# A sparse 3x3 convolution on one core: from a planned order to a hand-synchronised program with a loop on TensorE

## The chip, the cores and the metric

The kernel runs on one core of a Trainium2 chip. The metric is device time in microseconds of one execution. A core has TensorE (PE in the profile; its weight loads are PEld), VectorE (DVE), ScalarE (ACT), GpSimd (POOL) and SyncE (SP), each with its own instruction stream, and 16 DMA engines that all the transfers share. Engines wait for each other through semaphores. PSUM is the memory that TensorE writes, in eight banks of 2 KB a partition; SBUF is the working memory.

## The reference

A convolution of 16 images of 64 channels, 64 x 64 pixels, with 128 filters of 3 x 3, padded by one pixel, in fp32. A tenth of the weights are not zero, but the zeros lie at random.

```python
batch, c_in, h, w, c_out, k = 16, 64, 64, 64, 128, 3
x_pad = np.pad(x, ((0, 0), (0, 0), (pad, pad), (pad, pad)), mode='constant')
for b in range(batch):
    for co in range(c_out):
        for ci in range(c_in):
            for kh in range(k):
                for kw in range(k):
                    if weight[co, ci, kh, kw] != 0:
                        output[b, co] += weight[co, ci, kh, kw] * x_pad[b, ci, kh:kh+h, kw:kw+w]
```

## The kernel before

It treats the convolution as a dense one, in bf16 with fp32 sums. Two images are a pair: their 2 x 64 channels fill the 128 partitions, and the two halves of TensorE's rows work on one image each, side by side. So each step of the multiplication is two matmuls of 64 rows, one for each image.

A pair's 64 rows are cut into four blocks of 16 rows. A block of kind T (`twos`) saves a third of the work by sharing between two neighbouring rows of output. Write G0, G1, G2 for the three rows of taps. For output rows r and r+1, the sum x[r] + x[r+1] times G1 is needed by both; the even row adds x[r+1] times (G2 - G1) and x[r-1] times G0, the odd row adds x[r] times (G0 - G1) and x[r+2] times G2. So a block needs three products: shared (3 taps across), even (6) and odd (6), 15 pairs of matmuls on 8 rows of 64 columns. The first block of all is direct (D): 18 pairs, with no sum to wait for.

The engines share the work so: POOL adds the two rows (L169), TensorE multiplies (L150), ACT copies the shared product out of PSUM to `pc` (L176), and DVE adds it to the even and the odd product, once for each image, into the output tile `o` (L183). Tiles come from pools: eight PSUM tiles of one bank, three `s`, four `pc`, three `o`. A planner puts in the waits; the order on each engine is that in which the code is written (`manual_schedule`). The program is straight: TensorE has 989 matmuls and as many weight loads in its stream. Where a row above or below the image is wanted, the matmul is made one row shorter (441 or 448 columns instead of 504 or 512).

The start: SP loads the weights (L60) and the first 32 rows of pair 0 in fp32 (L62, `x_head`). DVE and ACT cast the weights to bf16 and the head too (L101), TensorE transposes the weights, and DVE forms the two differences. Idle matmuls fill TensorE's time before.

Loads of the other pairs are issued by POOL, which casts them to bf16 in the transfer (L63, L68). Up front go the rest of pair 0, pairs 1 to 3 and 24 rows of pair 4; the rest follow from inside the block loop, after the last sum of pairs 1 to 5, beside the stores. Stores are issued by SP as each pair is done (L207), the last pair's in two halves (L205). After pair 1's store five tiny loads of one weight (`spare`, L211) follow on SP.

Of the kernel before, what the change touches and what calls it, by code (L numbers as in the profile page):

```python
# [12 lines left out]

BLOCKS = {p: "TTTT" for p in range(8)}
BLOCKS[0] = "DTTT"  # L20


G0, G1, G2, G21, G01 = range(5)
KW_ORDER = (1, 0, 2)


@with_exitstack
def kernel(
# [7 lines left out]

# [4 lines left out]
    HEAD = 32  # L41

    const_pool = ctx.enter_context(tc.tile_pool(name="const", bufs=1))
    x_pool = ctx.enter_context(tc.tile_pool(name="x", bufs=1))
    s_pool = ctx.enter_context(tc.tile_pool(name="s", bufs=3))
    p_pool = ctx.enter_context(tc.tile_pool(name="pc", bufs=4))
    o_pool = ctx.enter_context(tc.tile_pool(name="o", bufs=3))
    psum_pool = ctx.enter_context(
        tc.tile_pool(name="psum", bufs=8, space=bass.MemoryType.PSUM)
    )  # L50

    ctx.enter_context(tc.manual_schedule())


# [3 lines left out]
    xs = [x_pool.tile([128, H, W], BF16, name=f"x{p}") for p in range(NP)]  # L58
    w_sb = const_pool.tile([C_OUT, C_IN * KH * KW], FP32, name="w_sb")
    nc.sync.dma_start(out=w_sb, in_=weight.rearrange("o i kh kw -> o (i kh kw)"))  # L60
    x_head = const_pool.tile([128, HEAD, W], FP32, name="x_head")
    nc.sync.dma_start(out=x_head, in_=pair(0)[:, 0:HEAD, :])  # L62
    nc.gpsimd.dma_start(out=xs[0][:, HEAD:H, :], in_=pair(0)[:, HEAD:H, :])  # L63
    ident = const_pool.tile([128, 128], BF16, name="ident")
    make_identity(nc, ident)

    def load(p, a=0, b=H):
        nc.gpsimd.dma_start(out=xs[p][:, a:b, :], in_=pair(p)[:, a:b, :])  # L68

    EARLY, CUT = 4, 24

    LATER = {2: (5,), 3: (6,), 4: (7, 0, 32), 5: (7, 32, 64)}
    for p in range(1, EARLY):
        load(p)
    load(EARLY, 0, CUT)


    idle_rhs = const_pool.tile([128, 512], BF16, name="idle_rhs")  # L80
    nc.vector.memset(idle_rhs, 0.0)  # L81
    idle_ps = psum_pool.tile([128, 512], FP32, name="ps")

    def keep_busy(n):
        for _ in range(n):
            nc.tensor.matmul(idle_ps, idle_rhs[:, 0:128], idle_rhs, start=True, stop=True)  # L86

    keep_busy(7)

    w_v = w_sb.rearrange("o (i k) -> o k i", k=KH * KW)
    w_bf = const_pool.tile([C_OUT, 3, 4 * C_IN], BF16, name="w_bf")
    w_bf4 = w_bf.rearrange("o g (k i) -> o g k i", k=4)
    wT = const_pool.tile([128, 5, 3, C_OUT], BF16, name="wT")
# [4 lines left out]
    def cast_x(copy, a, b):  # L100
        copy(out=xs[0][:, a:b, :], in_=x_head[:, a:b, :])  # L101

    def cast(g, copy, a, b):
        k = 3 * g + a % 3
        copy(out=w_bf4[:, g, a:b, :], in_=w_v[:, k : k + b - a, :])  # L105

    def transposed(g):
        wps = psum_pool.tile([128, 4, 128], FP32, name="ps")
        for j in range(3):
            src = w_bf[:, g, C_IN * j : C_IN * (j + 2)]  # L110
            nc.tensor.matmul(wps[:, j, :], src, ident, start=True, stop=True)  # L111
        return wps[:, 0:3, :]

    def difference(g, wps):
        nc.vector.tensor_tensor(out=wT[:, g], in0=wps, in1=wT[:, G1], op=SUB)  # L115

    cast(G1, nc.vector.tensor_copy, 0, 3)
    cast(G1, nc.scalar.copy, 3, 4)
    cast(G0, nc.vector.tensor_copy, 0, 3)
    cast(G0, nc.vector.tensor_copy, 3, 4)  # L120
    cast(G2, nc.scalar.copy, 0, 3)
    cast(G2, nc.vector.tensor_copy, 3, 4)
    cast_x(nc.vector.tensor_copy, 0, 9)
    nc.scalar.copy(out=wT[:, G1], in_=transposed(G1))
    ps0 = transposed(G0)
    nc.vector.tensor_copy(out=wT[:, G0], in_=ps0)  # L126
    ps2 = transposed(G2)
    nc.scalar.copy(out=wT[:, G2], in_=ps2)
    keep_busy(7)
    cast_x(nc.scalar.copy, 9, 18)  # L130
    difference(G01, ps0)
    difference(G21, ps2)
    cast_x(nc.scalar.copy, 18, HEAD)


    def product(terms, rows):


        ps = [psum_pool.tile([128, rows, W], FP32, name="ps") for _ in range(2)]
        todo = [(t, kw) for t in terms for kw in KW_ORDER]  # L140
        for i, ((src, g, first, step), kw) in enumerate(todo):
            n_src = src.shape[1]
            lo = 0 if first >= 0 else 1
            hi = rows if first + (rows - 1) * step < n_src else rows - 1
            c_lo, c_hi = max(0, 1 - kw), min(W, W + 1 - kw)
            a = first + lo * step
            b = first + (hi - 1) * step + 1
            for n in range(2):
                q = slice(64 * n, 64 * n + 64)
                nc.tensor.matmul(  # L150
                    ps[n][:, lo:hi, c_lo:c_hi],
                    tap(g, kw, n),
                    src[q, a:b:step, c_lo + kw - 1 : c_hi + kw - 1],
                    start=(i == 0),
                    stop=(i == len(todo) - 1),
                )
        return ps

    def direct(p, o, r0, rows):
        ps = product(  # L160
            [(xs[p], G1, r0, 1), (xs[p], G0, r0 - 1, 1), (xs[p], G2, r0 + 1, 1)], rows
        )
        nc.scalar.copy(out=o[0][:, r0 : r0 + rows, :], in_=ps[0])  # L163
        nc.vector.tensor_copy(out=o[1][:, r0 : r0 + rows, :], in_=ps[1])  # L164

    def twos(p, o, r0):
        t0 = r0 // 2
        s = s_pool.tile([128, 8, W], BF16, name="s")
        nc.gpsimd.tensor_tensor(  # L169
            out=s, in0=xs[p][:, r0 : r0 + 16 : 2, :], in1=xs[p][:, r0 + 1 : r0 + 16 : 2, :], op=ADD  # L170
        )
        shared = product([(s, G1, 0, 1)], 8)
        pc = []
        for n in range(2):
            c = p_pool.tile([128, 8, W], FP32, name="pc")
            nc.scalar.copy(out=c, in_=shared[n])  # L176
            pc.append(c)
        even = [(xs[p], G21, r0 + 1, 2), (xs[p], G0, r0 - 1, 2)]
        odd = [(xs[p], G01, r0, 2), (xs[p], G2, r0 + 2, 2)]
        for first, terms in ((r0, even), (r0 + 1, odd)):  # L180
            ps = product(terms, 8)
            for n in range(2):
                nc.vector.tensor_tensor(  # L183
                    out=o[n][:, first : r0 + 16 : 2, :], in0=ps[n], in1=pc[n], op=ADD
                )

    for p in range(NP):
        both = o_pool.tile([C_OUT, 2, H, W], FP32, name="o")
        o = [both[:, n] for n in range(2)]
        into = out[2 * p : 2 * p + 2].rearrange("n o h w -> o n h w")  # L190
        last = p == NP - 1
        for blk in range(4):
            r0 = 16 * blk
            if BLOCKS[p][blk] == "T":
# [47 lines left out]
```

## Time and profile before

| what | value |
|---|---|
| time, median of three runs | 131.87 us |
| the three runs | 126.64, 131.87, 132.14 us |
| span of the profiled execution, first to last instruction | 124.3 us |
| own total of the profiled execution | not given on the page; only the span is |
| TensorE busy | 108.7 us (87%) |
| DVE, ACT, POOL busy | 82.5, 39.0, 41.7 us |
| packets of SP's queue and of POOL's queue, share of 16 DMA engines | 67.2% and 30.7% |
| HBM read and written | 17.07 MB and 33.55 MB |

The page gives, for each group of instructions, its source line, engine, operation, output and input, count, then busy time in all, mean duration of one, and the idle time of the engine ahead of them with what ended it. The rows of tenths cut the span into 40 slices; a 9 means 90% or more. TensorE's busy time counts matmuls that overlap, so it says little of how near to its best it runs; the distance between equal steps says more.

### The profile page before, as it was taken

The numbers are of one execution on the slowest core, as the hardware profiler recorded it, in microseconds if no ns is written. First come the engines' busy times: TensorE is split into PE (matmuls) and PEld (weight loads), VectorE is DVE, ScalarE is ACT, GpSimd is POOL, SyncE is SP. The second block draws the span as 40 slices with busy tenths as digits, with TensorE's granted clock in tenths as the row PEclk, the third lists the DMA queues.
The fourth block names the chain that finished last, engine by engine and source line by source line (L and its number), as shares of the span: only waits on it lengthen the run. The fifth ranks groups of instructions, "written<-read, shape, count | busy, mean of one in ns | idle before, by whom it ended". The sixth has DMA issues, their size and how long they took to land.

```text
span 124.3 us, 2453 instructions
## 1 busy us (share of the span) xinstructions
PE 108.7 (87%) x989; PEld 57.2 (46%) x989; DVE 82.5 (66%) x135; ACT 39.0 (31%) x71; POOL 41.7 (34%) x47
## 2 busy tenths in 40 slices
PE   6959999999999999999999999999999999970000
PEld 2425555555555555555555555555555555530000
DVE  0353577877787778777877878887877787772000
ACT  4543333333333333333333333333333333330000
POOL 6409333533353335333443335333333320000000
PEclk9999999999999999999999999999999999997555
DMA  4999999999999999999999999999999999999991
GB/s 120 348 220 227 219 213 213 238 411 338 335 392 422 319 316 324 377 340 329 303 385 378 354 380 443 376 349 389 418 422 437 422 427 427 437 427 403 432 414 82
DMA packets 4198, 42.91 MB, mean 345 GB/s; under 512 B 347, under 2 KB 347, under 8 KB 1115
## 3 DMA queue, kind: packets, MB, share of 16 engines
q1 hardware_dynamic: 2746, 34.90, 67.2%
q0 software_dynamic: 1440, 7.86, 30.7%
q8 instruction: 7, 0.11, 0.3%
q14 instruction: 5, 0.03, 0.1%
HBM read 17.07 MB, written 33.55 MB: 407 GB/s over the span
## 4 chain that ended last, share of the span: by engine, by line
PE 82%; DMA 5%; DVE 1%; issue 1%; DVEq 0%; SPq 0%
PE ps L150 82%; DMA x_head<-in_x_dram 5%; DVE o L183 1%; DVEq L237 0%; DVE x L101 0%; SPq L60 0%; DVEq L183 0%
## 5 line engine op out<-in xcount | busy, mean ns | idle before, releaser
L183 DVE TENSOR_TENSOR o<-ps,pc 128x512 f32<-128x512 f32 x124 | 77.8, 686 | 22.1 <-PE ps L150 19.2
L150 PE MATMUL ps<-x,wT 64*128 64x504 bf16 (+3 forms) x780 | 88.8, 373 | 1.3 <-DVE x L101 1.3
L150 PEld LDWEIGHTS <-wT 64*128 64x128 bf16 x966 | 55.2, 94 | 49.5 <-issue 1.7
L169 POOL TENSOR_TENSOR s<-x 128x512 bf16<-128x512 bf16 x31 | 35.6, 1150 | 57.6 <-PE ps L150 41.1
L176 ACT COPY pc<-ps 128x512 f32<-128x512 f32 x62 | 33.3, 589 | 64.0 <-issue 61.8
L150 PE MATMUL ps<-s,wT 64*128 64x512 bf16 (+1 forms) x186 | 25.7, 377 | 0.0
L86 PE MATMUL ps<-idle_rhs 128*128 128x512 bf16 x14 | 4.8, 505 | 1.2 <-DVE idle_rhs L81 1.2
L68 POOL DMA_DIRECT2D x<-in_x_dram x9 | 5.0, 560 | 0.0
L86 PEld LDWEIGHTS <-idle_rhs 128*128 128x128 bf16 x14 | 1.5, 118 | 3.2 <-issue 1.4
L105 DVE CAST w_bf<-w_sb 128x192 bf16<-128x192 f32 (+1 forms) x4 | 1.1, 351 | 2.5 <-DMA w_sb<-in_weight_dram 2.5
L164 DVE COPY o<-ps 128x512 f32<-128x512 f32 x2 | 1.4, 692 | 2.0 <-PE ps L150 2.0
L101 DVE CAST x<-x_head 128x576 bf16<-128x576 f32 x1 | 0.5, 460 | 2.6 <-DMA x_head<-in_x_dram 2.6
L101 ACT CAST x<-x_head 128x576 bf16<-128x576 f32 (+1 forms) x2 | 1.5, 802 | 1.8 <-DMA x_head<-in_x_dram 1.8
L163 ACT COPY o<-ps 128x512 f32<-128x512 f32 x2 | 1.2, 586 | 2.4 <-PE ps L150 2.4
L105 ACT ACT_TABLE_LOAD x1 | 1.3, 1283 | 0.7 <-PEq L226 0.7
L105 ACT CAST w_bf<-w_sb 128x64 bf16<-128x64 f32 (+1 forms) x2 | 0.7, 416 | 1.6 <-DMA w_sb<-in_weight_dram 1.6
L115 DVE TENSOR_TENSOR wT<-ps,wT 128x384 bf16<-128x384 f32 x2 | 1.0, 548 | 0.0
L111 PEld LDWEIGHTS <-w_bf 128*128 128x128 bf16 x9 | 0.5, 97 | 1.0 <-DVE w_bf L105 1.0
L63 POOL DMA_DIRECT2D x<-in_x_dram x1 | 0.7, 693 | 0.8 <-POOLq L226 0.8
L111 PE MATMUL ps<-ident,w_bf 128*128 128x128 bf16 x9 | 0.9, 222 | 0.1
L81 DVE MEMSET idle_rhs<- 128x256 uint32 x1 | 0.3, 272 | 0.9 <-PEq L226 0.9
L126 DVE CAST wT<-ps 128x384 bf16<-128x384 f32 x1 | 0.6, 551 | 0.0
(8 smaller groups left out, 1.9 us busy)
## 6 DMA issues: line engine op xcount, KB each, us to landing
out_dram<-o SPq DMA_DIRECT2D x7, 4096.0 KB, 19.8
x<-in_x_dram POOLq DMA_DIRECT2D x5, 1024.0 KB, 16.8
out_dram<-o SPq DMA_DIRECT2D x2, 2048.0 KB
x<-in_x_dram POOLq DMA_DIRECT2D x3, 512.0 KB, 13.8
x_head<-in_x_dram SPq DMA_DIRECT2D x1, 1024.0 KB, 6.2
x<-in_x_dram POOLq DMA_DIRECT2D x1, 640.0 KB, 14.8
x<-in_x_dram POOLq DMA_DIRECT2D x1, 384.0 KB, 22.3
w_sb<-in_weight_dram SPq DMA_DIRECT2D x1, 288.0 KB
```

Source lines behind the costliest of these rows:

```text
L68: nc.gpsimd.dma_start(out=xs[p][:, a:b, :], in_=pair(p)[:, a:b, :])
L86: nc.tensor.matmul(idle_ps, idle_rhs[:, 0:128], idle_rhs, start=True, stop=True)
L101: copy(out=xs[0][:, a:b, :], in_=x_head[:, a:b, :])
L105: copy(out=w_bf4[:, g, a:b, :], in_=w_v[:, k : k + b - a, :])
L111: nc.tensor.matmul(wps[:, j, :], src, ident, start=True, stop=True)
L115: nc.vector.tensor_tensor(out=wT[:, g], in0=wps, in1=wT[:, G1], op=SUB)
L150: nc.tensor.matmul(ps[n][:, lo:hi, c_lo:c_hi], tap(g, kw, n), src[q, a:b:step, c_lo + kw - 1 : c_hi + kw - 1], start=(i == 0), stop=(i == ...
L163: nc.scalar.copy(out=o[0][:, r0 : r0 + rows, :], in_=ps[0])
L164: nc.vector.tensor_copy(out=o[1][:, r0 : r0 + rows, :], in_=ps[1])
L169: nc.gpsimd.tensor_tensor(out=s, in0=xs[p][:, r0 : r0 + 16 : 2, :], in1=xs[p][:, r0 + 1 : r0 + 16 : 2, :], op=ADD)
L176: nc.scalar.copy(out=c, in_=shared[n])
L183: nc.vector.tensor_tensor(out=o[n][:, first : r0 + 16 : 2, :], in0=ps[n], in1=pc[n], op=ADD)
```

## The change

The planner and its pools go. The whole program stands in one hand-written section, with named semaphores, and tiles with fixed addresses:

- TensorE's program becomes a loop of 16 turns over two blocks, counted by a register, with a branch at its end. Each product is preceded by waits that stand alone: `take` waits until a semaphore is at least 1 and lowers it by one. There are four for each block: `s_odd` and `s_sum` before the shared product, `s_free` before the even one, `s_even` before the odd one.
- So that all blocks look alike, the matmuls read fixed tiles. POOL still makes `sums`, and now also copies nine even rows of x (the block's and the next) to `even`; ACT copies nine odd rows (from the one above the block) to `odd`. Each tile is there twice. A row outside the image is written as zeros, so all blocks multiply full tiles. The direct first block is gone. For block 0 DVE fills both.
- PSUM: one tile of two banks for the shared product, one for the even, two in turn for the odd. ACT's copy and DVE's sums take both images in one instruction, of 1,024 elements a partition.
- The head of pair 0 stays fp32 and is loaded in two parts, 17 and 15 rows.
- Loads: POOL issues the rest of pair 0 and pairs 1 to 4 up front, and pairs 5 to 7 together after it has filled block 1's tiles.
- Stores: SP waits until pair 6 has landed (`GATE`) before the first store. Pairs 6 and 7 are stored in halves. There are four output tiles; the fourth (`home`) lies over the head and the tiles of pairs 0 to 2. The five `spare` loads are gone.

The waits of the other engines are written as counts of `s_pe`, which rises by two with each product, six with each block. The diff, cut to its core (added lines):

```diff
+    ctx.enter_context(tc.tile_critical(no_gpsimd_drain=True))
...
+    outs = [sbuf(f"o{k}", [C_OUT, 2, H, W], FP32) for k in range(3)]
+    outs.append(home.rearrange("o (n r) (h w) -> o n (r h) w", n=2, w=W))
...
+    sums = [sbuf(f"sums{k}", [128, HALF, W], BF16) for k in range(UNROLL)]
+    odd = [sbuf(f"odd{k}", [128, HALF + 1, W], BF16) for k in range(UNROLL)]
+    even = [sbuf(f"even{k}", [128, HALF + 1, W], BF16) for k in range(UNROLL)]
+    pc = [sbuf(f"pc{k}", [128, 2, HALF, W], FP32) for k in range(3)]
+    ps = [nc.alloc_psum_tensor(f"ps{k}", [128, 2, HALF, W], FP32).ap() for k in range(4)]
...
+    for i, (a, b) in enumerate(zip((0, FIRST), (FIRST, HEAD))):
+        nc.sync.dma_start(out=x_head[:, a:b, :], in_=pair(0)[:, a:b, :]).then_inc(s_head[i], 16)
...
+    fill_even(0, v, vcopy, vzero, s_dve)
+    fill_odd(0, v, vcopy, vzero, s_dve)
...
+    g = nc.gpsimd
+    for k in range(N):
+        if k >= UNROLL:
+            wait(g, s_pe, 6 * (k - UNROLL) + 2)
+        fill_sums(k)
+        if k == 0:
+            g.wait_ge(s_dve, 10)
+        else:
+            if k >= UNROLL:
+                wait(g, s_pe, 6 * (k - UNROLL) + 6)
+            fill_even(k)
+        if k == 1:
+            for p in range(UP_FRONT, NP):
+                load(p)
+
+    fill_odd(1)
+    for k in range(N):
+        wait(a, s_pe, 6 * k + 2)
+        a.copy(out=pc[k % 3], in_=ps[0]).then_inc(s_pc, 1)
+        if k + UNROLL < N:
+            wait(a, s_pe, 6 * k + 4)
+            fill_odd(k + UNROLL)
...
+    for k in range(N):
+        p, b = divmod(k, BLOCKS)
+        o = outs[p % 4]
+        r0 = ROWS * b
+        if p >= 4:
+            wait(v, s_st[p - 4], 16)
+        wait(v, s_pc, k + 1)
+        wait(v, s_pe, 6 * k + 4)
+        v.tensor_tensor(
+            out=o[:, :, r0 : r0 + ROWS : 2, :], in0=ps[1], in1=pc[k % 3], op=ADD
+        ).then_inc(s_free, 1)
+        wait(v, s_pe, 6 * k + 6)
+        v.tensor_tensor(
+            out=o[:, :, r0 + 1 : r0 + ROWS : 2, :], in0=ps[2 + k % 2], in1=pc[k % 3], op=ADD
+        ).then_inc(s_out, 1)
+
+    s = nc.sync
+    s.wait_ge(s_x[GATE], 16)
+    for p in range(NP):
...
+            s.wait_ge(s_out, BLOCKS * p + BLOCKS // parts * (h + 1))
+            s.dma_start(
+                out=into[:, :, rows * h : rows * (h + 1), :],
+                in_=outs[p % 4][:, :, rows * h : rows * (h + 1), :],
+            ).then_inc(s_st[p], 16)
...
+    def take(s):
+        t.wait_ge(s, 1).then_inc(s, -1)
...
+    nc.br("blocks", engines=[PE])
+    with nc.body("blocks", valid_engines=[PE]):
+        for k in range(UNROLL):
+            take(s_odd)
+            take(s_sum)
+            product(ps[0], [(sums[k], G1, 0)])
+            take(s_free)
+            product(ps[1], [(odd[k], G21, 1), (odd[k], G0, 0)])
+            take(s_even)
+            product(ps[2 + k], [(even[k], G01, 0), (even[k], G2, 1)])
+        t.reg_add(turn, turn, 1)
+        t.br_lt(turn, N // UNROLL, "blocks", "blocks_done")
```

## The prediction

> **What bounds the kernel now.** I read the page first, then the DMA view by stage, TensorE's timeline, and SP's waits.
>
> ```profile
> span 124.3 us, 2453 instructions
> ...
> DMA  4999999999999999999999999999999999999991
> GB/s 120 348 220 227 219 213 213 238 411 338 335 392 422 319 316 324 377 340 329 303 385 378 354 380 443 376 349 389 418 422 437 422 427 427 437 427 403 432 414 82
> ...
> q1 hardware_dynamic: 2746, 34.90, 67.2%
> q0 software_dynamic: 1440, 7.86, 30.7%
> q8 instruction: 7, 0.11, 0.3%
> ...
> PE 82%; DMA 5%; DVE 1%; issue 1%; DVEq 0%; SPq 0%
> ...
> L183 DVE TENSOR_TENSOR o<-ps,pc 128x512 f32<-128x512 f32 x124 | 77.8, 686 | 22.1 <-PE ps L150 19.2
> L150 PE MATMUL ps<-x,wT 64*128 64x504 bf16 (+3 forms) x780 | 88.8, 373 | 1.3 <-DVE x L101 1.3
> ...
> L169 POOL TENSOR_TENSOR s<-x 128x512 bf16<-128x512 bf16 x31 | 35.6, 1150 | 57.6 <-PE ps L150 41.1
> L176 ACT COPY pc<-ps 128x512 f32<-128x512 f32 x62 | 33.3, 589 | 64.0 <-issue 61.8
> ```
>
> The chain of work names TensorE for 82%, but it ends with the last instruction on a compute engine. The DMA row is the other story: nines from the second slice to the last but one. SP's waits show the end:
>
> ```profile
> SPq L237 <- DMA out_dram<-o: 10.0, 3, 4.8
> ```
>
> The last store is issued at 112.6 us and SP then waits 10.0 us for three store landings: a half store still lay ahead of it. So DMA ends the span, and TensorE (last matmul 111.2) is close behind.
>
> DMA rates by stage: the DMA view of 8 to 20 us (loads alone), then of 100 to 120 us (stores alone), then stages of 4 us, whose last two columns are the busy share and GB/s.
>
> ```profile
> DMA packets 367, 2.61 MB, mean 217 GB/s; under 512 B 47, under 2 KB 47, under 8 KB 53
> ```
>
> ```profile
> DMA packets 776, 8.47 MB, mean 424 GB/s; under 512 B 48, under 2 KB 48, under 8 KB 48
> ```
>
> ```profile
> 88.00:92.00 4.00, 4.00 (x40) 2.13 (x38) 3.27 (x6) 1.07 (x2) 1.15 (x1) 1.00 1.01 431
> ...
> 96.00:100.00 4.00, 4.00 (x42) 2.20 (x40) 3.06 (x5) 1.91 (x4) 1.92 (x2) 1.00 1.04 438
> ```
>
> A load is counted by the bf16 that it writes, so 217 GB/s is 434 GB/s of fp32 read.
>
> TensorE's pace, from its timeline: a block's shared product starts at 62.99, 66.23, 69.47, 72.63, that is 3.24 us for an inner block and 3.16 for one at an image's edge.
>
> ```profile
> 62.99 0.83 PE L150 MATMUL ps<-s,wT 64*128 64x512 bf16 x6
> 63.63 2.77 PE L150 MATMUL ps<-x,wT 64*128 64x512 bf16 x24
> 66.23 0.83 PE L150 MATMUL ps<-s,wT 64*128 64x512 bf16 x6
> ```
>
> **The change part by part.**
>
> *DMA order.* The same bytes move; no store starts before pair 6 has landed. Worked from pure rates: loads 7.86 MB / 0.217 = 36.2 us, stores 33.55 / 0.424 = 79.1, weights and head 3.6 (1.76 to 5.4 us is at a share of 1.00, and loads alone follow). Sum 118.9. First data come at 1.76, so DMA would be done at 120.7. Now it is done at about 121.8 (the stage 121.0 to 124.3 has a share of 0.24, 0.8 us). Gain 1.1 us. While SP waits for pair 6, pair 7 is still queued (1.05 MB / 0.217 = 4.8 us), more than the roughly 1 us from a store's issue to its first data (weights: issue 0.74, data 1.76), so no hole opens. The five spare DMAs go; SP's timeline has them from 36.2 to 41.1, with nothing due on SP before 48.6: 0.
>
> *Are stores there in time?* Output p is done at 8.2 + 12.96(p+1) + 1.3 (DVE's last sum), by the block time below. Pair 5: 87.3; DMA has by then loads to 41.6 and five stores of 9.9, so it wants pair 5 at 91. Pair 6's halves are done at 93.7 and 100.2, wanted at 101 and 106; pair 7's at 106.7 and 113.2, wanted at 111 and 116. Buffers: block 16 (at 60 us) overwrites output 0, stored by about 52. Enough.
>
> *TensorE's work.* Edge rows are now multiplied as zeros: 16 edge blocks go from 3.16 to 3.24. The direct first block (18 pairs of matmuls) becomes one of 15. So 32 x 3.24 = 103.7 us. The extra cost is 1.3 us for zeros less 0.6 for the first block.
>
> *The loop's waits.* Each block gets four waits that stand alone in TensorE's stream, and there are 16 branches. The trace has one such wait inside the stream: 51 ns, executed at 10.25 us, 2.2 us before the matmul it precedes (12.41), and the pair cadence of 0.216 goes on. The final drain, too, is reached 2.4 us before the last matmul ends. So the sequencer runs about ten pairs ahead and the waits cost nothing while that lead lasts. Bounds: 0, and 128 x 51 ns = 6.5 us. What the lead shrinks to depends on the last releaser. Odd tile: the block before's even product ends 1.94 into it, ACT copies 576 elements (672 ns in the x_head row), so 2.65 of 3.24; with the zero row (64 elements, 304 ns) 2.95. Even PSUM: DVE starts at 1.97 and takes two images at once (two of 686 ns overlap to 1.26, from 2.52 for four), so 3.23, wanted 0.65 into the next block. Lead 0.3 to 0.65 us, one and a half to three pairs. I take 0.5 us in all (nearest row: the 51 ns wait that cost nothing), and keep 6.5 as the end. Behind a late wait stand all further matmuls, then DVE, then the last store.
>
> *Helpers' budgets per 3.24 us.* ACT: one copy of 1024 (589 for 512 and 479 for 384 give 0.86 ns an element: 1.03 us) plus 0.67. DVE 2.5. POOL: 1.15 for the sum plus a copy of 576 elements, which the trace does not have: above, the two-input row scaled, 1.29; below, the 128-element memset, 0.22. Even with 1.29 it is 2.44. All are under 3.24, so off the path; if POOL's copy took over 2 us it would bound.
>
> *POOL's three late loads* stand between block 1's fill and block 2's sum: 3 x 0.56 = 1.7 us, from 10.2 to 11.9, then 1.15 to 13.1; wanted at 14.7. Cover 1.6 us. If an issue blocked because more is queued than before, block 2 would be late by the excess; no row shows one longer than 0.7 us.
>
> *Start.* x_head's casts (L101) become fills. DVE: weight differences end near 6.6, the two fills 0.46 and about 0.6, so 7.7. ACT needs the second head part, 7.4 as now, plus 0.67. TensorE starts at 8.2 (now 7.95). Entering the hand-written section adds a hop on SP ahead of the first DMA: 0.2 us; leaving it adds another round of drains: the round at the end now takes 0.9 after the last landing, so I add 0.4.
>
> *Sum.* TensorE ends at 8.2 + 103.7 + 0.5 = 112.4; DVE 113.7; data of the last half from 114.7 to 119.6. DMA by its own sum: 120.9. The later counts. The tail was 2.5 (121.8 to 124.3), now 2.9: span **123.8**, 0.5 us less (0.4%). Allowing half of the gap to the better DMA rates below, I forecast 0.8% less. The slack of TensorE is 1.3 us; past it each us is paid.
>
> The page gives no own total; the lowest run shown, 126.64, is 2.3 above the span, and the median, 131.87, is 7.6. I carry the ratio to the median: **130.8**.
>
> [...]
>
> **Rivals.** (1) *Unmixed traffic runs at the best stages.* Stores at 433 (77.5 us), loads at 219 (35.9), head 3.6: 117.0, done at 118.9, so TensorE then decides, at 119.6: span 122.5; with the 0.5 of the waits and the 0.4 of the way out both hidden 121.6, 2.2% less, 129.0. For: 88 to 100 us. Against: 424 over the long stretch. (2) *Waits exposed.* The lead is too short for the sequencer, and each stand-alone wait costs its 51 ns: TensorE ends at 118.4, data at 125.6, span 128.5, 3.4% more, 136.4. It costs from 1.3 us of exposure (10 ns a wait). For: the waits now empty the queue once a block; against: the wait at 10.25. [...] (4) *POOL late once*, by an issue that blocks for 3 to 5 us: span 125 to 128, about 134. (5) *The order does nothing*: stores and loads mix as well as they run apart (the 24 to 86 us stretch is busy at 1.02), span 124.7, same.
>
> **How the numbers follow.** Forecast 0.42, (5) 0.09, (1) 0.26, (2) 0.13, (3) 0.05, (4) 0.05. Faster by over 2%: 0.26; within 2% (about what a measurement of this kernel tells from nothing): 0.51; slower: 0.23. The range: up to case (2), 136.4; down to 2% under the lowest run shown, 124.1, since the median may fall at that level. The forecast's own span is 122.5 to 125.
>
> **What would show it.** Right: load-only DMA to about 42 us, then stores alone at 424 or more; TensorE's blocks 3.24 apart; an end set by the last store with the queue never empty. Wrong: gaps on TensorE at each block or each second one, a DMA share under 1 after 90 us, sums from POOL coming late at block 2.

## The result, and the profile after

| what | before | after |
|---|---|---|
| time, median of four runs each, side by side | 129.25 us | 132.09 us |
| lowest and highest run | 126.25 and 132.14 us | 130.94 and 133.41 us |
| time of the profiled execution | 126.64 us | 132.42 us |
| its span | 124.3 us | 130.7 us |
| TensorE's first product starts | 7.95 us | 14.61 us |
| last landing of a store | 123.44 us | 128.88 us |

The changed kernel is slower: the ratio is 1.042, with a 95% interval of 1.033 to 1.051. The kernel before shows its times at two levels (126.3 and 126.6, 131.9 and 132.1), and the ratio compares undisturbed runs alone, which for the kernel before are those of the lower level.

The 132.09 lies inside the range of the forecast, 124.1 to 136.4, but only because the forecast of 0.8% less was carried to the median of 131.87. Carried to the 126.64 of the profiled execution it would have been 125.6, with an upper end of 131.0 (the 3.4% of its second rival), and 132.42 came out. So the forecast was wrong, in sign and in size, and that the range held the result is luck. The span has 6.4 us to explain.

The page of the changed kernel:

```profile
span 130.7 us, 2483 instructions
...
PEclk9999559999999999999999999999999999999975
DMA  3999999999999999999999999399719999999692
GB/s 108 229 276 225 216 216 218 208 218 218 208 223 216 386 426 426 436 431 416 451 429 424 426 429 426 156 421 461 321 80 472 411 399 411 426 404 434 288 406 120
...
q1 hardware_dynamic: 3152, 34.90, 64.3%
q0 software_dynamic: 1152, 7.86, 29.0%
...
PE 81%; DVE 2%; issue 0%; DVEq 0%
...
L268 ACT COPY pc<-ps 128x1024 f32<-128x1024 f32 x32 | 32.4, 1012 | 42.0 <-PE ps L318 42.0
...
L284 DVE TENSOR_TENSOR o<-ps,pc 128x1024 f32<-128x1024 f32 x24 | 29.4, 1225 | 27.0 <-PE ps L318 27.0
...
L161 POOL COPY even<-x 128x576 bf16<-128x576 bf16 (+1 forms) x20 | 13.0, 649 | 21.4 <-PE ps L318 21.4
```

Three things are to be seen. The DMA row now has holes, from slice 26 on (82 us): before it was nines to the last slice but one. The clock row has a pair of fives in slices 5 and 6 (13 to 20 us). And the sizes that the forecast had estimated came out: ACT's copy 1.01 us (estimate 1.03), DVE's double sum 1.23 (1.26), POOL's copy 0.65 (between 0.22 and 1.29).

The loads run alone to about 42 us, the last of them lands at 46.4, and from there the stores run alone, at 416 to 451 GB/s, as was foreseen. Then the queue runs dry. That is SP's wait, by line 301, for DVE's sums; its wait for the last landings has shrunk from 10.0 us to 6.0:

```profile
SPq L301 <- DVE o L288: 53.8, 6, 12.7
...
SPq L306 <- DMA out_dram<-home: 6.0, 1, 6.0
```

So now the outputs are late, and TensorE decides the end. Its timeline (start, time from the first to the last of a group, in us; idle time ahead in brackets) shows where. The first line is the start of the kernel before, the rest is of the changed one:

```profile
7.95 3.99 PE L150 MATMUL ps<-x,wT 64*128 64x512 bf16 x36 [1.30 <-DVE x L101]
```

```profile
14.61 1.46 PE L318 MATMUL ps<-sums,wT 64*128 64x512 bf16 x6 [7.11 <-PEq L329]
15.85 2.79 PE L318 MATMUL ps<-odd,wT 64*128 64x512 bf16 x12
18.41 2.13 PE L318 MATMUL ps<-even,wT 64*128 64x512 bf16 x12
20.36 0.82 PE L318 MATMUL ps<-sums,wT 64*128 64x512 bf16 x6
...
23.60 0.82 PE L318 MATMUL ps<-sums,wT 64*128 64x512 bf16 x6
...
26.84 0.82 PE L318 MATMUL ps<-sums,wT 64*128 64x512 bf16 x6
```

The first product starts at 14.61, after 7.1 us in which TensorE did nothing. The first block takes 5.75 us (14.61 to 20.36), all others 3.24. This row of a stage gives the reason for the 5.75: the column before the last two is the granted clock, 0.56.

```profile
14.60:20.40 5.80, 5.79 (x32) 2.45 (x34) 1.23 (x1) 1.78 (x3) 3.86 (x7) 0.56 1.04 218
```

The sum is 14.61 + 5.75 + 31 x 3.24 = 120.8; DVE's last sum starts at 121.23. Against the forecast (start 8.2, 32 x 3.24, 0.5 for the waits: 112.4) this is 6.4 for the start and 2.5 for the clock, less the 0.5 that the waits did not take: 8.4. The forecast's own chain through TensorE ended with data at 119.6; 8.4 later is 128.0, and the last landing came at 128.88.

What did TensorE wait for? Not for block 0's own tiles: DVE has filled both by 10.27 us, and POOL's sum is done at 9.98. The wait named, L329, is `take`. Block 0's `take(s_odd)` is answered by ACT, and the first thing that ACT signals there is the fill of block 1's `odd` tile, which reads the odd rows 15 to 31, all but the first of them from the second part of the head. ACT's timeline, then the two parts in the view of the DMA issues (KB, us from issue to landing), then the whole head of the kernel before in the same view:

```profile
13.65 0.67 ACT L152 CAST odd<-home 128x576 bf16<-128x576 f32 x1 [7.34 <-DMA home<-in_x_dram]
```

```profile
home<-in_x_dram SPq DMA_DIRECT2D x1, 544.0 KB, 7.2
...
home<-in_x_dram SPq DMA_DIRECT2D x1, 480.0 KB, 11.7
```

```profile
x_head<-in_x_dram SPq DMA_DIRECT2D x1, 1024.0 KB, 6.2
```

So two things meet: a transfer of 480 KB that takes 11.7 us, where the whole head of 1,024 KB took 6.2 before, and a wait that is answered one block ahead. The trace's packets show why the transfer takes so long. The second part moves in 128 packets of 3,840 bytes, 162 ns each. From 4.96 us on POOL's loads are on the same DMA engines: first the rest of pair 0, whose packets write 4,096 bytes and take 322 ns, then pair 1, with 8,192 bytes and 624 ns. Fourteen of the sixteen engines have done their share by 10.5 us, the last at 13.56. Before, the head's packets were of 8,192 bytes, and when POOL's first packet came at 5.38, 96 of the 128 had ended. On the engine that is last, followed from packet to packet by start and end, packets of 162 and of 624 ns alternate from 10.34 to 12.63 us: the small ones start at 10.94, 11.70 and 12.47, so in that stretch the head gets 0.16 us of the engine's time in each 0.76.

### The profile page after: what moved, and what is told of

Read it like the earlier page. It is cut to its first block, busy times and chain, and to the rows that moved or that the text cites. A ratio compares the mean times of both kernels' runs of the same rounds, so it can differ in the third digit from the quotient of the medians.

```text
span 130.7 us, 2483 instructions
## 1 busy us (share of the span) xinstructions
PE 112.7 (86%) x983; PEld 56.2 (43%) x983; DVE 82.7 (63%) x75; ACT 57.1 (44%) x78; POOL 62.9 (48%) x86
## 4 chain that ended last, share of the span: by engine, by line
PE 81%; DVE 2%; issue 0%; DVEq 0%
PE ps L318 81%; DVE home L284 1%; DVE home L288 1%; DVEq L135 0%
## 5 line engine op out<-in xcount | busy, mean ns | idle before, releaser
L268 ACT COPY pc<-ps 128x1024 f32<-128x1024 f32 x32 | 32.4, 1012 | 42.0 <-PE ps L318 42.0
L318 PE MATMUL ps<-odd,wT 64*128 64x504 bf16 (+1 forms) x384 | 48.5, 385 | 0.0
L318 PE MATMUL ps<-even,wT 64*128 64x504 bf16 (+1 forms) x384 | 47.8, 381 | 0.0
L284 DVE TENSOR_TENSOR o<-ps,pc 128x1024 f32<-128x1024 f32 x24 | 29.4, 1225 | 27.0 <-PE ps L318 27.0
L318 PE MATMUL ps<-sums,wT 64*128 64x504 bf16 (+1 forms) x192 | 27.1, 384 | 7.1 <-PEq L329 7.1
L318 PEld LDWEIGHTS ps<-odd,wT 64*128 64x128 bf16 x384 | 21.7, 96 | 21.2 <-issue 2.0
L318 PEld LDWEIGHTS ps<-even,wT 64*128 64x128 bf16 x384 | 21.6, 96 | 20.9 <-issue 1.3
L288 DVE TENSOR_TENSOR o<-ps,pc 128x1024 f32<-128x1024 f32 x24 | 29.4, 1224 | 0.7 <-PE ps L318 0.6
L172 POOL TENSOR_TENSOR sums<-x 128x512 bf16<-128x512 bf16 x20 | 23.0, 1152 | 0.0
L318 PEld LDWEIGHTS ps<-sums,wT 64*128 64x128 bf16 x192 | 10.4, 95 | 17.8 <-issue 14.0
L172 POOL TENSOR_TENSOR sums<-home 128x512 bf16<-128x512 bf16 (+1 forms) x12 | 14.1, 1174 | 7.3 <-DMA home<-in_x_dram 7.2
L284 DVE TENSOR_TENSOR home<-ps,pc 128x1024 f32<-128x1024 f32 x8 | 9.8, 1224 | 6.3 <-PE ps L318 6.3
L288 DVE TENSOR_TENSOR home<-ps,pc 128x1024 f32<-128x1024 f32 x8 | 9.8, 1224 | 0.0
```

Of the source, the lines that this page charges most:

```text
L172: nc.gpsimd.tensor_tensor(out=sums[k % UNROLL], in0=src[:, r0 : r0 + ROWS : 2, :], in1=src[:, r0 + 1 : r0 + ROWS : 2, :], op=ADD,).then_in ...
L268: a.copy(out=pc[k % 3], in_=ps[0]).then_inc(s_pc, 1)
L284: v.tensor_tensor(out=o[:, :, r0 : r0 + ROWS : 2, :], in0=ps[1], in1=pc[k % 3], op=ADD).then_inc(s_free, 1)
L288: v.tensor_tensor(out=o[:, :, r0 + 1 : r0 + ROWS : 2, :], in0=ps[2 + k % 2], in1=pc[k % 3], op=ADD).then_inc(s_out, 1)
L318: mm = t.matmul(into[:, n, :, c_lo:c_hi], tap(g, kw, n), src[q, i : i + HALF, c_lo + kw - 1 : c_hi + kw - 1], start=(m == 0), stop=(m == l ...
```

## The experiments

All kernels but `before_split` are edits of the changed kernel. "Span" is that of the profiled execution; ratios are to the kernel before on the same chip, in the same series of runs.

| run | time, us | ratio (95%) | span | TensorE's first product | last landing |
|---|---|---|---|---|---|
| the changed kernel | 132.09 | 1.042 (1.033 to 1.051) | 130.7 | 14.61 | 128.88 |
| one_head | 129.16 | 1.026 (1.023 to 1.029) | 127.2 | 9.30 | 125.42 |
| own_odd | 129.47 | 1.030 (1.025 to 1.036) | 127.1 | 8.83 | 125.30 |
| loads_after_w | 129.40 | 1.030 (1.025 to 1.034) | 127.6 | 10.16 | 125.80 |
| warm | 130.26 | 1.033 (1.030 to 1.036) | 128.2 | 14.65 | 126.41 |
| before_split | 132.73 | 1.056 (1.052 to 1.060) | 129.5 | 7.32, its second half 12.80 | 128.17 |
| no_gate | 128.43 | 1.018 (1.011 to 1.026) | 126.6 | 9.27 | 124.86 |
| unrolled | 128.71 | 1.019 (1.011 to 1.027) | 127.6 | 9.26 | 125.83 |
| spread | 130.51 | 1.032 (1.024 to 1.041) | 128.8 | 9.74 | 127.07 |
| spread2 | 127.8 to 130.6 | none | 126.1 | 9.23 | 124.19 |

### The start

**one_head** undoes the split: the head is one DMA again.

```diff
-    for i, (a, b) in enumerate(zip((0, FIRST), (FIRST, HEAD))):
+    for i, (a, b) in enumerate(zip((0,), (HEAD,))):
...
-            return x_head, s_head[r >= FIRST]
+            return x_head, s_head[0]
```

> The changed kernel with the head of pair 0 as one load of 32 rows instead of 17 and 15; nothing else. Theory H (the late second part of the head is the whole loss: its packets of 3,840 B take turns with POOL's packets of 8,192 written bytes on the same DMA engines, so it lands at 13.6 us instead of 7.4): the head lands by 7.5 to 8, TensorE's loop starts at about 9.1 (both of VectorE's fills, 1.6 us, now stand behind the head) instead of 14.6, the first block takes 3.24 us instead of 5.7, TensorE ends near 113 instead of 121.2, span 122 to 124, time 124 to 126. Rival L (the loop, its waits or the store gate also cost several us that the late start hides): blocks longer than 3.3 us or holes in the stores appear, time 128 or more.

TensorE's timeline:

```profile
9.30 0.82 PE L318 MATMUL ps<-sums,wT 64*128 64x512 bf16 x6 [2.21 <-PEq L329]
...
12.54 0.83 PE L318 MATMUL ps<-sums,wT 64*128 64x512 bf16 x6
```

The head lands at 7.03, TensorE starts at 9.30, its first block takes 3.24, and DVE's last sum ends at 114.6, where the forecast had 113.7. Once the head is whole, TensorE's part of the forecast holds to within 1 us. But DVE's last sum is 7.8 us earlier than in the changed kernel (it starts at 113.41 instead of 121.23), and this buys only 3.5 us of span. The time stays 2.6% above the kernel before, 3 us and more over what was expected, without a block over 3.3 us and without a hole in the stores. So neither of the two expectations fits: something else holds the end, and it is taken up below.

**loads_after_w** keeps the two parts and takes the contention away: POOL's loads are issued only when the weights have landed.

```diff
+    nc.gpsimd.wait_ge(s_w, 16)
     load(0, HEAD, H)
```

> The changed kernel, the head still in two parts, but POOL waits for the weights (landed at 3.9 us) before it issues its first load, so that its packets start some 2.5 us later. Theory H (taking turns with POOL's packets): the second part is through before POOL's packets begin, at 7 to 8 us; TensorE starts at 8.5 to 9, ends near 113, time 125 to 127. Rival R (rows cut into 4,352 and 3,840 B are slow whatever runs beside them): the second part still lands after 10 us, TensorE starts after 11, time over 128.5.

The same 480 KB, in the same packets, take half the time, and ACT hardly waits for them:

```profile
home<-in_x_dram SPq DMA_DIRECT2D x1, 480.0 KB, 5.7
```

```profile
7.67 0.67 ACT L153 CAST odd<-home 128x576 bf16<-128x576 f32 x1 [0.31 <-DMA home<-in_x_dram]
```

It was the sharing that made the second part late (11.7 against 5.7 us), not its short rows. (TensorE starts at 10.16 here, later than expected, because POOL also makes `ident` later, from 5.35 instead of 2.61 us, and the transposes wait 1.13 us for it. The time, 129.40, is over the expected 125 to 127 as in `one_head`.)

**before_split** does that one part of the change alone, in the kernel before.

```diff
-    nc.sync.dma_start(out=x_head, in_=pair(0)[:, 0:HEAD, :])
+    for lo, hi in ((0, 17), (17, HEAD)):
+        nc.sync.dma_start(out=x_head[:, lo:hi, :], in_=pair(0)[:, lo:hi, :])
```

> The kernel before with its head load cut into the same two parts, rows 0 to 16 and 17 to 31. Theory H (any kernel with POOL's loads queued beside the second part loses): the second part lands at 10 to 14 us; ScalarE's cast of rows 9 to 17 and with it the second half of the direct block waits for it, TensorE ends 3 to 6 us later, time 129 to 132 for a run that is otherwise at 126.5. Rival (the split hurts only in the new program): the head lands near 7.5 and the time is that of the kernel before within 1%.

```profile
7.32 2.04 PE L151 MATMUL ps<-x,wT 64*128 64x512 bf16 x18
12.80 3.81 PE L151 MATMUL ps<-x,wT 64*128 64x512 bf16 x18 [3.44 <-ACT x L102]
```

The second part lands 10.3 us after its issue and ACT casts at 12.08. TensorE does the first half of its first block at 7.32, on the first part alone, and begins the second half at 12.80, after 3.4 us without work; in the kernel before both halves run on end from 7.95 to 11.94. The second half is also slow, 3.81 us for 18 matmuls, at a granted clock of 0.54 from 12.8 to 16.4 us. The 5.6% are more than the whole change costs, so nothing else in the change is needed for a late start.

**warm** leaves the late start and keeps TensorE busy until then.

```diff
     transposed(G2)
-    keep_busy(7)
+    keep_busy(39)
```

> The changed kernel with 39 instead of 7 idle matmuls after the transposes, so that TensorE is busy until about 14 us; the head still lands at about 13.6. Theory C (about 2.5 us of the loss is the granted clock, which stands at 0.5 of full from 13 to 19.6 us after TensorE's 7.1 us of idleness): the loop starts at about 14.6 to 15, its first block takes 3.24 us, TensorE ends 2 to 2.5 us earlier, time about 129.5 to 130. Rival: the slow first block has another cause (late tiles from POOL or ACT): it stays near 5.7 us and the time near 132.

```profile
14.65 0.82 PE L318 MATMUL ps<-sums,wT 64*128 64x512 bf16 x6 [0.40 <-PEq L329]
...
17.89 0.83 PE L318 MATMUL ps<-sums,wT 64*128 64x512 bf16 x6
```

The start is the same, and the first block takes 3.24 instead of 5.75. So the second cost of the late head, 2.5 us on TensorE, is the clock, which had gone to about half in the 7.1 us of idleness; the profiled span falls by as much, 130.7 to 128.2, and the median time by 1.8. In the changed kernel the granted clock is a half from 12.9 to 19.7 us, that is until 5.1 us after the work begins, and full after that; in `warm` it is 1.00 from 12 to 20.4 us.

**own_odd** leaves the split and the contention, and takes away the coupling of block 0 to block 1's tile. TensorE begins with a credit of its own; ACT copies a block's shared product first and then fills the next block's `odd`, so that the wait on `s_odd` still guards the PSUM tile of the shared product.

```diff
-    fill_odd(1)
     for k in range(N):
         wait(a, s_pe, 6 * k + 2)
         a.copy(out=pc[k % 3], in_=ps[0]).then_inc(s_pc, 1)
-        if k + UNROLL < N:
-            wait(a, s_pe, 6 * k + 4)
-            fill_odd(k + UNROLL)
-        else:
-            a.copy(out=w_bf[:, 0, 0:1], in_=zeros[:, 0:1]).then_inc(s_odd, 1)
+        if k + 1 < N:
+            if k >= 1:
+                wait(a, s_pe, 6 * (k - 1) + 4)
+            fill_odd(k + 1)
...
     t.sem_inc(s_even, 1)
+    t.sem_inc(s_odd, 1)
```

> In the changed kernel the wait of block 0 on `s_odd` is answered by ACT's fill of block 1's `odd` tile, which reads the second part of the head; DVE has both of block 0's tiles at 10.27. This kernel keeps the head in two parts and lets TensorE begin with a credit of its own; ACT copies a block's shared product first and then fills the next block's `odd`, so the wait still orders the PSUM tile. If that wait carries the late part over to block 0: TensorE starts at 10.6 to 10.9 at full clock (it is idle for about 3 us only), block 1 starts when POOL's second sum is there (14.96 in the changed kernel), so near 15.0, and the last product is 5.3 us earlier, near 115.7; the DMA queue is then never empty after 44 us, the last store lands near 125.5 to 126, and the time is 129 to 130, as with the head in one piece. If the late second part alone is enough, whatever waits for it (POOL's sums, too, stand behind it): start near 14.6 and 132.

```profile
8.83 0.83 PE L316 MATMUL ps<-sums,wT 64*128 64x512 bf16 x6 [0.90 <-PEq L327]
...
13.86 0.82 PE L316 MATMUL ps<-sums,wT 64*128 64x512 bf16 x6 [1.61 <-PEq L327]
...
17.36 0.82 PE L316 MATMUL ps<-sums,wT 64*128 64x512 bf16 x6
```

The second part still takes 10.4 us from issue to landing and ACT still casts it at 12.39, but block 0 now runs meanwhile, at the full pace: its second product starts 0.64 us after its first, where it is 0.65 in `one_head` and 1.24 at half the clock in the changed kernel. (Whether 3 us without work would have left the clock whole, as expected, was not shown: TensorE stood idle for 0.90 us only.) DVE's last sum starts at 114.99, and the time is that of `one_head`, inside what was expected. So the late part reaches block 0 through the one wait that is answered a block ahead; without that wait the split costs TensorE 1.6 us ahead of block 1, and the time nothing that can be seen. (The first part landed earlier here than in the changed kernel, 5.0 us after its issue against 7.2, so the start is better than expected.)

Three different cures of the start end at 129.2 to 129.5, 2.6 to 3.0% above the kernel before. What is left has another cause.

### The end

In `one_head` DVE is done at 114.6 and SP then waits for DMA alone, 9.7 us:

```profile
SPq L306 <- DMA out_dram<-home: 9.7, 1, 9.7
```

By the trace's packets fifteen DMA engines land the last store by 122.30 us, and one lands at 125.42. The last one falls behind store by store: of the first store fifteen landings are in by 53.94 and the last at 54.12, of the sixth fifteen by 102.71 and the last at 105.45. In 12 us of stores 18 to 21 of some 313 packets of 16 KB are slow, taking 630 ns or more; that is one packet in 16. They take 647 ns on average, the others 611. (The packets carry no engine's number; that the slow ones belong to the late engine is read from their number and from how its lag grows.) Beside loads (`no_gate`, 32 to 56 us) none is slow, and in `one_head` none after the arithmetic has ended. In the kernel before there are 2 to 8 in the mixed stages and 14 to 20 in the unmixed one at the end (92 to 116 us).

**unrolled** asks whether the loop has a part in it: `one_head` with its 32 blocks written straight, with the same waits.

```diff
...
-    with nc.body("blocks", valid_engines=[PE]):
-        for k in range(UNROLL):
...
-        t.br_lt(turn, N // UNROLL, "blocks", "blocks_done")
...
+    for k in range(N):
...
```

> The changed kernel with the head in one load and TensorE's 32 blocks written out straight, with the same waits, no register and no branch. Theory: the loop costs nothing (its blocks are 3.24 us apart, like the kernel before), and the instructions that must now be fetched cost next to nothing: 129.2 us within 0.5. Rival F (branches back cost time that shows only in the end, or TensorE's straight program slows the DMA): a difference of over 1 us either way.

128.71 against 129.16, on intervals that overlap, and as expected: the loop and its branches cost nothing that can be seen. They do save something that does not count here. The page of the straight kernel, then that of `one_head`, among the DMA queues:

```profile
q8 instruction: 7, 0.11, 0.3%
```

```profile
q14 instruction: 3, 0.02, 0.0%
```

With the straight program seven instruction packets of 16 KB move on queue 8, which take 879 to 1,008 ns each, and in its last store seven engines land between 122.91 and 123.21, behind eight that land by 122.09. In `one_head` none of queue 8 moves (the three of 8 KB on queue 14 are in both), so they are taken here for the instructions of TensorE, the only program in which the two kernels differ. But the sixteenth engine is last in both, at 125.83 and 125.42. So it is not the fetching of TensorE's instructions that makes it late.

**no_gate** is `one_head` without SP's wait for pair 6, so stores and loads mix.

```diff
-    s.wait_ge(s_x[GATE], 16)
```

> The changed kernel with the head in one load (129.2 us, its last store landing at 125.4 us, one of the 16 DMA engines some 3.5 us behind the others) and without the wait for pair 6 ahead of the first store, so that stores of the first pairs run beside the loads of the later ones. Theory M (in an unmixed run of stores one DMA engine needs some 648 ns for each packet of 16 KB where the others need 611, so its lag grows by 0.55 us with each store; beside loads it doesn't lag): the lag at the end shrinks by about 1 to 1.5 us for the two or three stores that move beside the loads, time 127.5 to 128.3. Rival P (unmixed order is the faster one, and the lag grows anyway): time 129 or more. TensorE should not wait, since pair 4 lands by 40 us and is wanted at 61.

128.43, a little over the expected 127.5 to 128.3; the slow engine is 2.2 us behind (124.86 against 122.62) instead of 3.1. The intervals of this run and of `one_head` overlap, so the gain in time is not shown by itself. **spread** also holds pairs 4 to 7 back, to be issued after blocks 7, 11, 15 and 19.

```diff
-    UP_FRONT = 5
+    UP_FRONT = 4
...
-        if k == 1:
-            for p in range(UP_FRONT, NP):
-                load(p)
+        if k in (7, 11, 15, 19):
+            load(UP_FRONT + (k - 7) // 4)
```

> As the kernel without the gate, and loads 4 to 7 issued by POOL after blocks 7, 11, 15 and 19, about as the kernel before has them, so that loads and stores are mixed until about 85 us. Theory M: the lag grows in the last four stores alone, to 2 to 2.5 us as in the kernel before; time 126 to 127, within 1% of the kernel before. Rival P: 129 or more. Rival Q (the remaining loss lies in the program's start and end, not in the DMA order): 128.5 to 129.5 whatever the loads do.

The slow engine is only 1.4 us behind, but the page's DMA row shows that the queue ran short in the slices 8, 12 and 13, and the time missed the expected 126 to 127, at 130.51 (130.1 to 135.4):

```profile
GB/s 112 350 230 209 214 221 216 122 453 407 326 203 173 432 382 315 338 348 384 323 341 343 389 328 336 331 427 432 437 417 437 437 397 432 420 435 425 432 320 8
```

**spread2** is `no_gate` with the loads at the times of the kernel before.

```diff
-    UP_FRONT = 5
-    for p in range(1, UP_FRONT):
+    CUT = 24
+    for p in range(1, 4):
         load(p)
+    load(4, 0, CUT)
+    LATER = {6: (4, CUT, H), 10: (5,), 14: (6,), 18: (7, 0, 32), 22: (7, 32, H)}
...
-        if k == 1:
-            for p in range(UP_FRONT, NP):
-                load(p)
+        if k in LATER:
+            load(*LATER[k])
```

> The changed kernel with the head in one load, no gate, and the loads at the times of the kernel before: up front the rest of pair 0, pairs 1 to 3 and 24 rows of pair 4, then the rest of pair 4, pairs 5 and 6 and the halves of pair 7 after POOL's blocks 6, 10, 14, 18 and 22 (about 23, 36, 49, 62 and 75 us). Theory M' (mixing keeps the slow engine level, and the kernel with late loads lost 1.5 us only through holes in the DMA stream, 122 GB/s at 23 us and 173 to 203 at 36 to 42): no hole, the last engine within 2 us of the others, time 126 to 127. Rival Q (something else in the new program costs the 3 us): 128.5 or more with a full DMA stream.

Its four runs took 127.8, 128.0, 130.5 and 130.6 us, which is too far apart for a ratio. The profiled one, 127.98, is 1.2% above the kernel before (126.41) and 1 us over what was expected. Its lag is 1.1 us (124.19 against 123.09), there is no hole, and 1.9 us pass from the last landing to the end of the span, where the kernel before takes 0.9. As far as this run and the one beside it at 127.8 tell, the order of the loads is worth about half of what is left, and the way out of the hand-written section most of the other half; this is argued from the traces and not shown by a ratio.

What makes the engine slow? Six kernels leave all of the convolution out. **dry** only loads, and then stores eight outputs of zeros. The others add one kind of idle work beside it: 70 DVE sums of 1,024 (**dry_dve**), 80 ACT copies and 80 POOL sums (**dry_act_pool**), 420 matmuls of 512 columns over all rows (**dry_pe**), or 860 matmuls of 64 rows in pairs, one in 0.106 us, which is the pace of the real blocks (**dry_pe2**); **dry_all** is the last with DVE, ACT and POOL busy too. The core of these edits:

```diff
+    for p in range(NP):
+        s.wait_ge(s_x[p], 16)
...
+        s.dma_start(out=into, in_=outs[p % 3]).then_inc(s_st[p], 16)
...
+    for k in range(860):                      # dry_pe2 and dry_all
+        n = k % 2
+        q = slice(64 * n, 64 * n + 64)
+        nc.tensor.matmul(
+            flat[1][:, n, :], idle_rhs[q, 0:128], idle_rhs[q, :], start=True, stop=True
+        )
```

> The loads and the stores alone: the same loads, then eight stores of 4 MB one behind the other from three tiles of zeros, with all arithmetic left out, so that no compute engine runs beside the stores. Theory B (the slow engine is slowed by what the compute engines do beside it): nearly no packet of 16 KB takes over 630 ns, and the 16 engines' landings of the last store lie within 1.5 us of each other. Theory I (this engine is slower by itself in an unmixed run): one packet in 16 takes about 648 ns and the spread grows by 0.55 us a store to over 4 us.

> Loads and stores alone as in the run without arithmetic, and beside them 70 sums on VectorE of 1,024 elements (PSUM and SBUF in, SBUF out, as in the kernel, at about 1.22 us each, until about 113 us); the output is zeros. If VectorE's work slows the one DMA engine: about one packet of 16 KB in 16 takes 640 ns or more from 45 to 113 us, and the last landing lags by 0.4 to 0.55 us more with each store. If not: all packets 611 to 628 ns, the landings of a store within 0.3 us, as without arithmetic.

> The same with 80 copies of 1,024 elements from PSUM on ScalarE and 80 sums of 512 bf16 on POOL instead (about 1.05 and 1.15 us each, to about 112 and 120 us). If ScalarE's or POOL's work slows the one DMA engine: one packet in 16 at 640 ns or more and a growing lag; if not, all packets 611 to 628 ns.

> The same with 420 matmuls of 128 x 512 on TensorE instead (0.216 us each, from about 21 to 112 us). If TensorE's work (or the fetch of its instructions) slows the one DMA engine: one packet in 16 at 640 ns or more and a growing lag; if not, all packets 611 to 628 ns.

> Loads and stores alone, all arithmetic of the kernel left out, and beside them 860 matmuls of 64 rows in pairs on TensorE, at the rate of instructions of the kernel itself (0.106 us each, twice that of the run with 420 matmuls). If the rate of TensorE's instructions slows the one DMA engine: one packet of 16 KB in 16 at 640 ns or more, and a last landing 3 us behind the others. If not: all at 611 to 628 ns, with a lag under 2 us as in the run with 420.

> The same with those matmuls, 70 sums on VectorE, 70 copies on ScalarE and 70 sums on POOL together, all arithmetic of the kernel left out. If it takes all the engines together: one packet in 16 at 640 ns or more between 45 and 100 us, none after the engines have ended, and a lag of about 3 us. If not: the slow engine comes from something else in the program (its semaphores, the tiles that it stores from), and stays open.

| run | time of the one run, us | span | slow 16-KB packets in 12 us (630 ns or more), of about 310 | of these 640 ns or more | TensorE's instruction packets | landings of the last store, first to last, us |
|---|---|---|---|---|---|---|
| dry | 126.83 | 125.1 | none | none | none | 0.18 |
| dry_act_pool | 126.97 | 125.2 | none | none | none | 0.35 |
| dry_dve | 127.47 | 125.7 | 0 to 1 | none | none | 0.64 |
| dry_pe | 128.58 | 126.8 | 3 to 5 | 1 to 2 | 3 | 1.96 |
| dry_pe2 | 130.08 | 128.0 | 21 to 22 | 8 to 9 | 6 | 2.39 |
| dry_all | 130.39 | 128.6 | 21 to 22 | 10 to 14 | 6 | 2.90 |

The counts are of the three stretches of 12 us from 81 to 117 us. Before that all six runs have slow packets of another kind: a third of those in the first 12 us of stores, and about one on each engine between 69 and 81 us. In `one_head` 15 to 18 of the slow packets take 640 ns or more.

The page's DMA row of `dry`, and its rates from 84 to 96 us beside those of `dry_pe2`:

```profile
DMA  3999999999999599999999999999999999999991
...
84.00:96.00 12.00, 0.00 (x0) 0.00 (x0) 1.00 1.01 430
```

```profile
84.00:96.00 12.00, 12.00 (x114) 5.32 (x112) 0.00 (x0) 0.00 (x0) 1.00 0.99 418
```

In these stretches, with TensorE idle or with the other engines busy, at most one packet is slow. With TensorE at 420 long matmuls a few are, and at the blocks' rate of some 19 matmuls and weight loads a microsecond as many as in the real kernel, though fewer of them reach the 640 ns that was expected. The other engines add no more of them. (`dry` and `unrolled`, which has 19 from 81 to 93 us, ran on the same chip.) So the slow packets come with TensorE's work. Whether its rate of instructions decides, or the kind of matmul (all rows in `dry_pe`, half of them, in pairs, in `dry_pe2`), was not separated.

The lag is another matter. It was expected to be 3 us, and it came to 2.4 in `dry_pe2` and 2.9 in `dry_all`, but in another way: in the three runs with TensorE one engine is some 2 us late from the first store on, and at the end several are, while in `one_head` a single one falls behind step by step. Their TensorE program is straight, and in `dry_pe` an instruction packet at 49.21 us takes 961 ns, and the three store packets around it 945, 907 and 975 ns instead of 615, which is 1.9 us in all. So the widths in the last column are in part those of instruction packets, which `one_head` does not have, and they do not show that the slow packets alone make a lag of 3 us. What carries the slow packets is open; no run shows whether the taking of the profile has a share in them. These are single runs; the runs of the kernel before that stand beside some of them lie between 125.55 and 126.61, and the packet counts are plainer than the times.

`dry` also gives the floor of the order "all loads, then all stores": a span of 125.1, with a hole of 1.5 us between the last packet of a load (42.70) and the first of a store (44.17), which the real kernel need not have. Without it the floor is, as an estimate, 123.6, beside 124.3 of the whole kernel before.

## Why the prediction was wrong, by its steps

*DMA order: rates as forecast, and worth nothing.* Loads and stores ran apart at the foreseen rates. In `one_head` fifteen of sixteen engines are done by 122.30, where the forecast had 120.7 and the kernel before its last landing at 123.44; but the span waits for the sixteenth, 3.1 us later. The working took a mean rate of all engines over a stage, and the end is set by the slowest one. The rows could have said so: the landings of the last store of the kernel before are spread over 2.1 us (121.30 to 123.44), and the forecast, which put the end of DMA at 121.8, read that as a tail that would stay.

*Start: the step that failed.* It said "ACT needs the second head part, 7.4 as now, plus 0.67". The dependency was right; the time was that of a different transfer, a head in one piece. The second part landed at 13.56, 6.2 us later, and block 0 waits for it, though none of its tiles needs it. The cold clock, 2.5 us, was not in the working at all. Besides, DVE's two fills take 0.75 and 0.89 us where 0.46 and 0.6 stood: in `one_head`, with the head on time, TensorE starts at 9.30, not 8.2. "Past it each us is paid" was right: the slack was 1.3 us, and 8.4 us came.

*TensorE's work and the loop's waits: right.* 31 blocks at 3.24 us, with four waits of 51 ns and every second time a branch: 0 for them, the lower bound, where 0.5 was taken. Rival (2), exposed waits, falls with this. The 0.05 under (3), a part of the 0.23 for slower, is for time lost at the 16 branches back, and no run shows a branch that costs time: the blocks are 3.24 us apart with a branch between them and without, and `unrolled`, which has none, took 128.71 us beside the 129.16 of `one_head`, on intervals that overlap. A DMA share under 1 after 90 us, named as a sign of being wrong, did come (0.49 from 92 to 96 us), but from the late start and not from the waits.

*Helpers and POOL's loads: right.* All three sizes came within 0.1 us of the estimates or inside the bounds, and the three late loads take 1.64 us (1.7) and hold nobody up in the changed kernel or in `one_head`. Rival (4) falls.

*Rival (1), the best rates throughout:* stores alone did run at 416 to 451 GB/s in the changed kernel, but no DMA queue decides its end; and in `one_head`, where it does, the slow engine takes that gain and more. *Rival (5), no worth in the order,* came nearest on this point: by `no_gate` and `spread2`, mixing is if anything better.

*The way out:* 0.4 us were added; it is 0.9 to 1.0. The hop at the entry, 0.2, is right (first DMA issued at 0.95 instead of 0.74).

*The carry to the median* laid the ratio on 131.87, while the span it was worked out on belongs to a run of 126.64. Its range held the result for that reason alone.

Of the 6.4 us of span, 3.5 go when the head is whole again; of the other 2.9, 2.0 lie in the later last landing and 0.9 in the way out.

## What to carry to other kernels

When a load that the start waits for is cut, each part is a transfer of its own: price it by its packets and by what else is queued at that moment, not by the landing of the whole (here 11.7 us for 480 KB, where the whole 1,024 KB took 6.2). Follow each counted wait to the instruction that answers it: a wait that is answered one turn ahead was harmless here in the steady state (blocks 3.24 us apart) and brought the second block's late input, landed at 13.56 us, to the first block's start, 14.61. And where DMA sets the end, look at the landings of the sixteen engines one by one, since a mean rate hides the one that is late (by 3.1 us in `one_head`).

## What had not been expected of the hardware

- In `one_head` one packet in 16 of the stores is 6% slower (647 against 611 ns for 16 KB) while TensorE executes some 19 instructions a microsecond (114 matmuls and 114 weight loads from 84 to 96 us); none is beside loads (`no_gate`, 32 to 56 us) or, from 81 us on, without TensorE (`dry`). In `one_head` one engine ends 3.1 us behind the others.
- A packet of TensorE's instructions, of 961 ns, and three slow store packets around it cost one DMA engine 1.9 us in the middle of stores (`dry_pe`).
- 480 KB in packets of 3,840 bytes took 11.7 us beside POOL's loads, whose packets write 4,096 and 8,192 (the changed kernel), and 5.7 without them (`loads_after_w`).
- In the changed kernel, after 7.1 us without work, TensorE's first block ran at a granted clock of 0.56, and 5.1 us of work passed before the clock was whole again, at a price of 2.5 us; after 3.4 us without work it was 0.54 in `before_split` (12.8 to 16.4 us), and after 2.2 us in `one_head` 1.00 (8 to 12 us).
- A loop's branch back over some 130 instructions, 16 times, cost nothing that the trace shows: its blocks are 3.24 us apart, as the inner blocks are in the kernel before, which has no branch.
